# Eight modulation vectors of the first layer: half of their products moved from VectorE to TensorE

## The chip, the cores and the metric

The kernel runs on one core of a Trainium2 chip. The metric is device time in microseconds: the median over several executions of one launch. An engine is named as in the profile: PE is TensorE's matmul, PEld its weight load, DVE is VectorE, ACT is ScalarE, POOL is GpSimd, SP is SyncE, which only issues DMAs here.

## The reference

Two transformer-like blocks of two layers each run one after the other on x, 256 tokens by 1024 channels, all in float32. What matters here is the beginning of the first block. From a conditioning vector c (1024 numbers) it makes, per layer, six vectors of 1024 that shift, scale and gate the activations:

```python
c_act = jax.nn.silu(c)
for layer in range(DEPTH):
    mod = c_act @ ada_w[layer] + ada_b[layer]
    shift1, scale1, gate1, shift2, scale2, gate2 = jnp.split(mod[:, None, :], 6, axis=-1)
    h = rms_norm(x, norm_mix[layer]) * (1.0 + scale1) + shift1
    ...
    y = mixer_conv_hgrn(h, w_in_ab[j], ...)
```

`ada_w[layer]` is 1024 x 6144, so each of the six vectors is the product of a vector with a 1024 x 1024 matrix. `scale1` and `shift1` of layer 0 are needed before anything else of the network can start: the first projection (`w_in_ab`) takes h.

## The kernel before, in words

The activations lie transposed, 8 blocks of 128 channels (partitions) by 256 tokens. All weights come as a stream of 1 MB units, 128 x 2048 float32, in an order written out by `weight_plan`; six buffers `raw` take them. SP issues the loads in that order (`pump`), each when its buffer is given back (`release`), so a late release also holds up every load behind it. An ordinary weight unit is split in two before use: ACT rounds it to `wh` (type fp32r), DVE subtracts to get the rest `wl` (line 314), and PE does three products for each pair of blocks with the activations, which are split likewise into XH and XL (all matmuls stand at line 337, all ACT operations at 294).

The units of `ada_w` are not split. A modulation unit (l, p, h) holds 256 of the 1024 outputs of vector p of layer l; vector 1 is `scale1`, vector 0 is `shift1`, and h counts from 0 to 3. The host lays it out transposed, output on the partition, 1024 inputs along the row, twice (j = 0, 1). `ada_dot` (line 688) multiplies one half by `crow`, c_act spread over all partitions (it lies in the tile adaacc), and sums along the row: one DVE instruction of 128 x 1024 gives one column of 128 outputs, `mod[l, p][:, 2h + j]`, and a tiny one reads the accumulator. `crow` itself is made by PE at the start (`ada_row`).

The stream begins with the eight units of layer 0 that the first projection needs, (0,1,0) to (0,1,3), then (0,0,0) to (0,0,3); the first weight unit, hf 0, goes ahead of the last of them. I call these units 0 to 7. In `layer0_mixer` a loop of eight steps, whose order on DVE and ACT is kept as written, goes through them: step i calls `ada_next()` (both halves of unit i), then `arrived(i)`: for units 0 to 3 ACT scales two blocks by `scale1` (tiles tq, tb), for units 4 to 7 ACT adds `shift1` and rounds to two blocks of XH (tile X); `rest(i)` makes the two blocks of XL on DVE. Before the loop stand the sums of squares on PE (`stats`), the root on ACT (tiles lnvt, rsbt) and two DVE multiplications of x by it (tiles g and sg). In step 7, `unit_hi` puts ACT's rounding of hf 0 (wh) between the XH of unit 6 and that of unit 7. The first projection on PE starts with that wh:

```python
for i in range(8):
    if i == 7:
        lo = self.unit_hi()
    self.ada_next()
    if i:
        rest(i - 1)
    arrived(i)
```

Later modulation units (48 in all) are put between later work in the same way; they are not touched by the change.

Of the kernel before, what the change touches and what calls it, by code (L numbers as in the profile page):

```python
# [10 lines left out]
F32 = mybir.dt.float32  # L11
F32R = mybir.dt.float32r
U8 = mybir.dt.uint8
AF = mybir.ActivationFunctionType
# [9 lines left out]
D = 1024  # L24
NK = D // 128
# [14 lines left out]

DMALO = ()
S5SEQ = "g P0 P1 g T0 T1 TB0 M0 P2 P3 TB1 Q0 Q1 T2 T3 g Q2 Q3"


# [2 lines left out]
def weight_plan():  # L49
    plan = []  # L50

    def cols(key, name, index, c0, n):
        for u in range(n // 256):
            plan.append(("w", (key, u), ("cols", name, index, [(c0 + u * 256, 256)])))

    def rows(key, name, index, r0, n):
        for u in range(n // 256):
            plan.append(("w", (key, u), ("rows", name, index, r0 + u * 256)))

    def ada(l, p):  # L60
        return [("ada", ("ada", l, p, h), ("ada", l, p, h)) for h in range(4)]

    def mlp(tag, w1, w2, l, extra):
        a, b = [], []
        for u in range(DFF // 256):
            a.append(("w", (tag + "a", u), ("cols", w1, l, [(u * 256, 256)])))
            b.append(("w", (tag + "b", u), ("rows", w2, l, u * 256)))
        if tag in COLS2:
            plan.extend(a + [("w", (tag + "b", u), ("tcol", w2, l, u // 2, u % 2)) for u in range(len(a))])
            return  # L70
        n = len(a)
        order = [a[0]]
        for u in range(1, n - 1):
            order += [a[u], b[u - 1]]
        order[-1:] = [a[n - 1], b[n - 3]]
        order += [b[n - 2], b[n - 1]]
        extra = list(extra)
        out = []
        for i, o in enumerate(order):
            out.append(o)  # L80
            if i >= 2 and i % 2 == 0 and extra:
                out.append(extra.pop(0))
        plan.extend(out + extra)

    plan.extend(ada(0, 1) + ada(0, 0))
    more = ada(0, 2) + ada(0, 4) + ada(0, 3)
    for i, (n, c0) in enumerate((("hf", 2048), ("hg", 3072), ("hq", 1536), ("hi", 2560),
                                 ("ac", 512), ("ah", 1024), ("ab", 0))):
        for u in range(2):
            plan.append(("w", (n, u), ("cols", "w_in_ab", 0, [(c0 + u * 256, 256)])))  # L90
            if i:
                plan.append(more.pop(0))
    plan.insert(7, plan.pop(8))
    rows("wab", "w_out_ab", 0, 0, D)
    mlp("m1", "mlp_w1", "mlp_w2", 0, ada(0, 5) + ada(1, 1) + ada(1, 0))
    def unit(name, u, w, index, *c):
        plan.append(("w", (name, u), ("cols", w, index, [(x, 256 // len(c)) for x in c])))

    for u in range(2):
        unit("v", u, "w_qkv", 0, 2 * D + u * 256)  # L100
    more = ada(1, 3) + ada(1, 4) + ada(1, 2)
    for i in range(12):
        if i < 8:
            unit("qk", i, "w_qkv", 0, i * 128, D + i * 128)
        elif i < 10:
            unit("v", i - 6, "w_qkv", 0, 2 * D + (i - 6) * 256)
        else:
            plan.append(("w", ("wc", i - 10), ("rows", "w_out_c", 0, (i - 10) * 256)))
        plan.extend(more.pop(0) for _ in range(SBA[i]))
    for i in range(2, 4):  # L110
        plan.append(("w", ("wc", i), ("rows", "w_out_c", 0, i * 256)))
    mlp("m2", "mlp_w1", "mlp_w2", 1, ada(1, 5))
    glu = [("w", ("glu", m), ("cols", "ssm_w_glu_2", 0, [(m * 128, 128), (D + m * 128, 128)])) for m in range(NK)]
    for k in S5SEQ.split():
        plan.append(glu.pop(0) if k == "g" else ("s5", (k[:-1], int(k[-1])), None))
    plan.extend(glu)
    mlp("m3", "mlp_w1_2", "mlp_w2_2", 0, [])
    cols("k", "w_kvf_2", None, 0, D)
    plan.append(("w", ("f", 0), ("fcols",)))
    for n, u in (("fq", 0), ("fv", 0), ("fq", 1), ("fq", 2), ("fq", 3), ("fv", 1), ("fv", 2), ("fv", 3)):  # L120
        unit(n, u, *(("attn_wq_2", 0, u * 256) if n == "fq" else ("w_kvf_2", None, D + u * 256)))
    rows("wo", "attn_wo_2", 0, 0, D)
    mlp("m4", "mlp_w1_2", "mlp_w2_2", 1, [])
    return plan
# [149 lines left out]
class Prog:  # L274
# [122 lines left out]
    def unit_ahead(self, ahead, between=None):  # L397

        last = min(self.used_n + ahead, len(self.wseq) - 1)
        while self.split_n <= last:  # L400
            j = self.wseq[self.split_n]
            if j not in self.slot:
                assert self.split_n > self.used_n, ("not loaded", self.plan[j][1])
                break
            b = self.split_n % len(self.hb)
            raw = self.raw_of(j)
            if self.plan[j][1] in DMALO:
                self.act(self.hb[b], raw, AF.Copy)
                self.release(j)
                lo = self.lb[b]  # L410
                self.act(lo, self.hb[b].bitcast(F32), AF.Copy, scale=-1.0)
                self.nc.gpsimd.dma_start(out=lo, in_=self.a["wst"][self.wpos[j]], accum_op=ADD)
                self.split_n += 1
                continue
            n = 1 + (self.plan[j][1][0] in HALVES)
            parts = [slice(i * 2048 // n, (i + 1) * 2048 // n) for i in range(n)]
            for c in parts:
                self.act(self.hb[b][:, c], raw[:, c], AF.Copy)
            if between is not None:
                between()  # L420
                between = None
            for c in parts:
                self.tt(self.lb[b][:, c], raw[:, c], self.hb[b][:, c].bitcast(F32), SUB)
            self.release(j)
            self.split_n += 1
        if between is not None:
            between()
# [76 lines left out]
                wh, wl = (t[:, k, m * 128:(m + 1) * 128] for t in (hv, lv))  # L504
                self.pair(outs[m], wh, wl, self.X2[S][:, k], k == 0, k == NK - 1)

    def rows_mm(self, units, xs, banks, start, stop, evac=None, late=False):

        kt = [(h, l, j) for h, l in units for j in range(2)]
        out = lambda m: self.pb[banks[m // 2]][:, (m % 2) * T:(m % 2 + 1) * T]  # L510
        if evac is not None:
            fin, a, b = evac
        if late:
            for q, m in [(q, m) for q in range(2) for m in range(NK)]:
                h, l, j = kt[q]
                w = h[:, j * D + m * 128:j * D + (m + 1) * 128]
                self.mm(out(m), w, xs[q][0], q == 0 and start and m % 2 == 0, False)
                self.mm(out(m), w, xs[q][1], False, False)
            for q, m in [(q, m) for q in range(2) for m in range(NK)]:
                h, l, j = kt[q]  # L520
                self.mm(out(m), l[:, j * D + m * 128:j * D + (m + 1) * 128], xs[q][0], False, q == 1 and stop and m % 2 == 1)
            return
        for m in range(NK):
            o = out(m)
            for q, (h, l, j) in enumerate(kt):
                c = j * D + m * 128
                xh, xl = xs[q]
                wh, wl = h[:, c:c + 128], l[:, c:c + 128]
                self.mm(o, wh, xh, q == 0 and start and m % 2 == 0, False)
                self.mm(o, wh, xl, False, False)  # L530
                self.mm(o, wl, xh, False, q == len(kt) - 1 and stop and m % 2 == 1)
            if evac is not None and m % 2 == 1:
                for i in (m - 1, m):
                    fin(i, out(i))
                    a(i)
                    if i:
                        b(i - 1)
        if evac is not None:
            b(NK - 1)
# [144 lines left out]
    def ada_dot(self, l, p, m, w):  # L684
# [3 lines left out]
        self.nc.vector.tensor_tensor_reduce(out=w, in0=w, in1=self.crow, scale=1.0 if sc is None else sc, scalar=b, op0=MUL, op1=ADD,  # L688
                                            accum_out=self.mod[l, p][:, m:m + 1])

    def ada_affine(self, l, p, m):
        c = l * 48 + p * 8 + m
        if p not in (1, 4):
            return None, self.adab[:, c:c + 1]
        return self.P["norm_mix" if p == 1 else "norm_mlp", l][:, m:m + 1], self.adn[l, p][:, m:m + 1]

    def ada_next(self, n=2):

        with self.tc.high_priority(offset=-BACK["ada"]):
            for _ in range(n):  # L700
                (l, p, h) = self.ada_todo[0]
                i = self.pos["ada", l, p, h]
                j = self.ada_k % 2
                w = self.raw_of(i)[:, j * D:(j + 1) * D]
                self.ada_dot(l, p, 2 * h + j, w)
                self.ada_k += 1
                if j:
                    self.release(i)
# [243 lines left out]
    def mlp(self, tag, S, finish, side=(), after=None, before=None):  # L952
        n = DFF // 256
        with self.tc.tile_pool(name="pm" + tag, bufs=1) as p:
# [22 lines left out]
            def B(us, fin=None):  # L977
                ws = [self.unit((tag + "b", u), ahead=2 - i) for i, u in enumerate(us)]
                xs = [(hh[u % 3][:, j, :], hl[u % 3][:, j, :]) for u in us for j in range(2)]
                self.rows_mm(ws, xs, yb, us[0] == 0, us[-1] == n - 1, fin, (tag + "b", us[0]) in DMALO)  # L980

            def sides(b):
                self.side_banks = (b, b + 1)
# [847 lines left out]
```

## Time and profile before

| what | value |
|---|---|
| median of 3 runs | 1312.97 us (1312.78 to 1313.27) |
| the profiled execution's own time | 1311.48 us |
| its span, first to last instruction | 1309.7 us |
| PE busy | 1225.6 us, 94% of the span |
| DVE busy | 1021.1 us, 78% |
| ACT busy | 681.8 us, 52% |
| mean granted TensorE clock | 0.98 |

The busy shares are means over stages with different limits. The clock is given in shares of full speed: 1.00 is the level of 2.4 GHz, 0.50 that of 1.2 GHz. A matmul in float32 shows as two records, each with a weight load of its own (8 matmuls are x16 in the trace). In a timeline the first number is the start, the second how long the row lasted, xN how many instructions it merges, and the bracket tells what ended the idle time before it.

### The profile page before, as it was taken

What the parts mean: (1) busy time and instruction counts of PE and PEld (TensorE: products, weight loads), DVE (VectorE), ACT (ScalarE), POOL (GpSimd) and SP (SyncE); (2) the same over time, 40 slices, a digit from 0 to 9 for tenths busy, and PEclk for the clock granted to TensorE, in tenths of its full rate; (3) what the DMA queues carried; (4) which work ended last, traced back from release to release, by engine and by line L of the source; (5) the groups of instructions that cost most, each with busy time, mean ns of one, the idle gap of its engine ahead of it and who ended that gap; (6) DMA issues with size and microseconds to landing.
All of it is one profiled execution on the core that took longest, in us unless ns stands there. A gap on an engine that the chain in (4) does not pass through costs nothing.

```text
span 1309.7 us, 22500 instructions
## 1 busy us (share of the span) xinstructions
PE 1225.6 (94%) x9412; PEld 1138.2 (87%) x9412; DVE 1021.1 (78%) x1398; ACT 681.8 (52%) x884; POOL 85.5 (7%) x73
## 2 busy tenths in 40 slices
PE   2999999999999999978889789999999999999997
PEld 2999899999988899978889579887889999888886
DVE  6899999985899969979956857676657786887553
ACT  4545465555548857534555345544545554655442
POOL 0012120000100001000000204000000000100000
PEclk7899999999999999989999899999999999999999
DMA  9867467778365567667579895444555533455520
GB/s 382 325 259 287 201 253 274 279 276 297 131 243 212 205 242 248 249 212 253 180 265 233 233 336 210 160 162 172 214 193 193 193 130 114 156 185 189 213 77 33
DMA packets 63654, 283.84 MB, mean 217 GB/s; under 512 B 8000, under 2 KB 25920, under 8 KB 31936
## 3 DMA queue, kind: packets, MB, share of 16 engines
q1 hardware_dynamic: 63552, 282.40, 60.6%
q8 instruction: 74, 1.21, 0.4%
q14 instruction: 28, 0.23, 0.0%
HBM read 267.70 MB, written 14.68 MB: 216 GB/s over the span
## 4 chain that ended last, share of the span: by engine, by line
PE 68%; DVE 16%; ACT 8%; DMA 4%; issue 3%; POOL 1%; DVEq 0%; ACTq 0%; SPq 0%; POOLq 0%
PE psall L337 67%; DVE wl L314 6%; ACT wh L294 5%; DVE raw L688 2%; DMA raw<-dK 2%; DMA raw<-in_wst_dram 1%; PE psall L340 1%; DMA raw<-dP 1%; DVE tmpn L327 1%; DVE sqt L327 1%; DVE X L327 1%; DVE td L314 1%; POOL sqat L566 1%; DVE sqt L314 0%; ACT X L294 0%
## 5 line engine op out<-in xcount | busy, mean ns | idle before, releaser
L337 PE MATMUL psall<-X,wh 128*128 128x256 f32 (+2 forms) x3360 | 729.3, 308 | 39.7 <-ACT wh L294 23.3
L337 PEld LDWEIGHTS psall<-X,wh 128*128 128x128 f32 x3360 | 544.6, 192 | 78.8 <-ACT wh L294 24.0
L337 PE MATMUL psall<-X,wl 128*128 128x256 f32 (+1 forms) x1992 | 559.2, 284 | 5.9 <-DVE wl L314 5.9
L314 DVE TENSOR_TENSOR wl<-raw,wh 128x2048 fp32r<-128x2048 f32 (+1 forms) x232 | 426.6, 1856 | 108.7 <-ACT wh L294 108.3
L294 ACT ACTIVATE wh<-raw 128x2048 fp32r<-128x2048 f32 (+1 forms) x232 | 354.3, 1546 | 217.3 <-PE psall L337 193.4
L337 PEld LDWEIGHTS psall<-X,wl 128*128 128x128 f32 x1992 | 378.0, 190 | 12.1 <-DVE wl L314 11.3
L337 PE MATMUL psall<-hh,wh 128*128 128x256 f32 x512 | 144.5, 287 | 4.4 <-ACT hh L294 4.3
L337 PE MATMUL psall<-hl,wh 128*128 128x256 f32 x512 | 145.6, 285 | 1.0 <-DVE hl L314 0.9
L337 PE MATMUL psall<-hh,wl 128*128 128x256 f32 x512 | 145.0, 284 | 0.0
L337 PE MATMUL psall<-hid,wh 128*128 128x512 f32 (+1 forms) x432 | 136.3, 372 | 0.0
L566 POOL TENSOR_TENSOR sqat<-sqat,sqt 128x256 f32<-128x256 f32 x52 | 56.2, 1081 | 1054.0 <-ACT sqt L294 1052.9
L337 PE MATMUL psall<-hid,wl 128*128 128x256 f32 x384 | 108.2, 282 | 0.2 <-DVE wl L314 0.2
L337 PEld LDWEIGHTS psall<-hh,wh 128*128 128x128 f32 x512 | 98.0, 193 | 5.6 <-ACT hh L294 5.1
L337 PEld LDWEIGHTS psall<-hl,wh 128*128 128x128 f32 x512 | 98.5, 192 | 1.5 <-DVE hl L314 1.5
L337 PEld LDWEIGHTS psall<-hh,wl 128*128 128x128 f32 x512 | 98.6, 193 | 0.4 <-issue 0.4
L337 PEld LDWEIGHTS psall<-hid,wh 128*128 128x128 f32 x432 | 78.1, 189 | 15.3
L688 DVE CUSTOM_DVE_ANT_0 raw<-raw,adaacc,prmt 128x1024 f32<-128x1024 f32 x64 | 81.4, 1294 | 0.0
L337 PEld LDWEIGHTS psall<-hid,wl 128*128 128x128 f32 x384 | 72.8, 189 | 0.6 <-DVE wl L314 0.6
L294 ACT ACTIVATE tmpn<-psall 128x256 f32<-128x256 f32 (+1 forms) x38 | 17.7, 465 | 62.1 <-PE psall L337 62.1
L314 DVE TENSOR_TENSOR tmpn<-tmpn,psall 128x256 f32<-128x256 f32 (+1 forms) x32 | 17.6, 552 | 38.0 <-ACT tmpn L294 38.0
L688 DVE CUSTOM_DVE_ANT_0 raw<-raw,adaacc,adn 128x1024 f32<-128x1024 f32 x32 | 42.3, 1340 | 4.4 <-ACT td L294 4.4
L294 ACT ACTIVATE ht<-ht 128x512 f32<-128x512 f32 x64 | 40.0, 626 | 6.2 <-DVE ht L327 5.3
(344 smaller groups left out, 1239.6 us busy)
## 6 DMA issues: line engine op xcount, KB each, us to landing
raw<-in_wst_dram SPq DMA_DIRECT2D x231, 1024.0 KB, 4.9
dQ<-s5X SPq DMA_DIRECT2D x8, 512.0 KB, 5.1
dP<-s5X SPq DMA_DIRECT2D x16, 256.0 KB, 3.9
s5X<-in_wst_dram SPq DMA_DIRECT2D x4, 1024.0 KB, 14.8
raw<-dK SPq DMA_DIRECT2D x32, 128.0 KB, 8.4
s5X<-in_s5blk_dram SPq DMA_DIRECT2D x8, 256.0 KB, 3.5
s5X<-dP SPq DMA_DIRECT2D x2, 1024.0 KB, 8.1
raw<-dP SPq DMA_DIRECT2D x2, 1024.0 KB, 12.0
```

Of the source, the lines that this page charges most:

```text
L294: i = self.nc.scalar.activation(out=out, in_=in_, func=func, **kw)
L314: return self.nc.vector.tensor_tensor(out=out, in0=a, in1=b, op=op)
L327: return self.nc.vector.scalar_tensor_tensor(out=out, in0=a, scalar=s, in1=b, op0=op0, op1=op1)
L337: return self.in_bank(out, self.nc.tensor.matmul(out, lhsT=l, rhs=r, start=start, stop=stop))
L340: return self.in_bank(out, self.nc.tensor.transpose(out, in_, self.ident))
L566: self.nc.gpsimd.tensor_tensor(out=self.sqa, in0=self.sqa, in1=s, op=ADD)
L688: self.nc.vector.tensor_tensor_reduce(out=w, in0=w, in1=self.crow, scale=1.0 if sc is None else sc, scalar=b, op0=MUL, op1=ADD, accum_out= ...
```

## The change

Units 0, 2, 4 and 6, that is h = 0 and h = 2 of vectors 1 and 0 of layer 0, go to PE. The host lays them out like ordinary weights, 8 blocks of 128 inputs by 256 outputs. For each half, `ada_mm` does eight float32 matmuls, the weights 128 x 128, the moving operand one column of `cact`, summed in one column of PSUM bank 5, and an ACT instruction of 128 x 1 brings the sum to `mod` with the same scale and bias that `ada_dot` used. Units 1, 3, 5 and 7 stay on DVE. The lines on `DMALO` and `late` remove code that did not run, since `DMALO` was empty.

```diff
-DMALO = ()
+ADAPE = {(0, p, h) for p in (0, 1) for h in (0, 2)}
...
     def ada(l, p):
-        return [("ada", ("ada", l, p, h), ("ada", l, p, h)) for h in range(4)]
+        return [("ada", ("ada", l, p, h), ("cols", "ada_w", l, [(p * D + h * 256, 256)]) if (l, p, h) in ADAPE
+                 else ("ada", l, p, h)) for h in range(4)]
...
+    def ada_mm(self, l, p, m, w):
+
+        sc, b = self.ada_affine(l, p, m)
+        o = self.pb[5][:, 8 * p + m:8 * p + m + 1]
+        for k in range(NK):
+            self.mm(o, w[:, k, :], self.cact[:, k:k + 1], k == 0, k == NK - 1)
+        self.act(self.mod[l, p][:, m:m + 1], o, AF.Identity, scale=sc, bias=b)
+
...
                 j = self.ada_k % 2
-                w = self.raw_of(i)[:, j * D:(j + 1) * D]
-                self.ada_dot(l, p, 2 * h + j, w)
+                if (l, p, h) in ADAPE:
+                    self.ada_mm(l, p, 2 * h + j, self.raw_of(i).rearrange("p (k c) -> p k c", c=256)[:, :, j * 128:(j + 1) * 128])
+                else:
+                    self.ada_dot(l, p, 2 * h + j, self.raw_of(i)[:, j * D:(j + 1) * D])
```

How the instructions stand on two engines shows what waits for what. The first place is PE between the sums of squares (td, tw) and the first projection (X, wh). Before:

```order
L337 MATMUL psall<-td,onesd 128x256 [waits Activation_49] x4
L337 MATMUL psall<-tw,onesd 128x256 [waits Activation_49] x4
L337 MATMUL psall<-X_171,wh_73 128x256 [waits Activation_49]
L337 MATMUL psall<-X_171,wh_73 128x256 [waits DVE_49]
L337 MATMUL psall<-X_171,wh_73 128x256 x3
```

And now (raw_67 is the buffer of unit 0, raw_69 that of unit 2, raw_71 that of unit 4; lines are shifted by one):

```order
L338 MATMUL psall<-td,onesd 128x256 [waits Activation_49] x4
L338 MATMUL psall<-tw,onesd 128x256 [waits Activation_49] x4
L338 MATMUL psall<-cact,raw_67 128x1 [waits DMAHW3_49]
L338 MATMUL psall<-cact,raw_67 128x1 x7
L338 MATMUL psall<-cact,raw_67 128x1 [waits Activation_49]
L338 MATMUL psall<-cact,raw_67 128x1 x7
L338 MATMUL psall<-cact,raw_69 128x1 [waits DMAHW5_49,Activation_49]
L338 MATMUL psall<-cact,raw_69 128x1 x7
L338 MATMUL psall<-cact,raw_69 128x1 [waits Activation_49]
L338 MATMUL psall<-cact,raw_69 128x1 x7
L338 MATMUL psall<-cact,raw_71 128x1 [waits DMAHW7_49,Activation_49]
```

Eight groups of eight matmuls now stand there, two to a unit, and from the second on each group waits for an ACT instruction, the one that reads the group before it out of the same PSUM bank.

The second place is ACT from the root to the rounding of hf 0 (wh_73). Before:

```order
L294 ACTIVATE lnvt<-psall,epscols 128x256 [waits PE_49]
L294 ACTIVATE rsbt<-lnvt 128x256 [waits Activation_49]
L307 ACT_TABLE_LOAD
L294 ACTIVATE tq<-g_181,mod_1_117 128x256 [waits DVE_49]
L294 ACTIVATE tq<-g_181,mod_1_117 128x256
L294 ACTIVATE tq<-g_181,mod_1_117 128x256 [waits DVE_49] x2
L294 ACTIVATE tb<-sg,mod_1_117 128x256 [waits DVE_49] x4
L294 ACTIVATE X_171<-tq,mod_0_116 128x256 [waits DVE_49,Activation_49] x4
L294 ACTIVATE X_171<-tb,mod_0_116 128x256 [waits DVE_49,Activation_49] x2
L294 ACTIVATE wh_73<-raw_68 128x2048 [waits DMAHW2_49]
```

And now, from the root on:

```order
L295 ACTIVATE mod_1_117<-psall,adn_1_128,prmt 128x1 [waits PE_49]
L295 ACTIVATE rsbt<-lnvt 128x256 [waits Activation_49]
L308 ACT_TABLE_LOAD
L295 ACTIVATE mod_1_117<-psall,adn_1_128,prmt 128x1 [waits PE_49]
L295 ACTIVATE tq<-g_181,mod_1_117 128x256 [waits DVE_49]
L295 ACTIVATE tq<-g_181,mod_1_117 128x256 [waits Activation_49]
L295 ACTIVATE tq<-g_181,mod_1_117 128x256 [waits DVE_49] x2
L295 ACTIVATE mod_1_117<-psall,adn_1_128,prmt 128x1 [waits PE_49] x2
L295 ACTIVATE tb<-sg,mod_1_117 128x256 [waits Activation_49] x2
L295 ACTIVATE tb<-sg,mod_1_117 128x256 [waits DVE_49] x2
L295 ACTIVATE mod_0_116<-psall,prmt 128x1 [waits PE_49] x2
L295 ACTIVATE X_171<-tq,mod_0_116 128x256 [waits Activation_49] x2
```

The first of the new instructions, for unit 0, stands ahead of rsbt; the pair for unit 2 stands behind all four tq; a further pair, for unit 6, stands behind the four X of tq, and the two X of tb and wh_73 follow it. On DVE the dots of units 0, 2, 4 and 6 are gone and the rest keeps its order: g and sg, then units 1, 3 and 5, four XL, unit 7, four XL, then wl. On SP the loads keep their order; those that reuse the buffers of units 0, 2, 4 and 6 now wait for PE where they waited for DVE.

## Rows read from the trace of the kernel before

**Rows 1.** The page: span, busy time, PE and its clock in 40 slices.

```profile
span 1309.7 us, 22500 instructions
...
PE 1225.6 (94%) x9412; PEld 1138.2 (87%) x9412; DVE 1021.1 (78%) x1398; ACT 681.8 (52%) x884; POOL 85.5 (7%) x73
...
PE   2999999999999999978889789999999999999997
...
PEclk7899999999999999989999899999999999999999
```

**Rows 2.** The chain that ended last, 14 to 36 us: start, us, what.

```profile
14.27 0.48 ACT lnvt L294
...
14.77 0.42 ACT rsbt L294
...
15.22 1.23 DVE g L314
...
33.30 0.51 ACT X L294
33.81 1.81 ACT wh L294
...
35.66 0.58 PE psall L337
```

**Rows 3.** The groups of instructions on DVE, 0 to 36 us.

```profile
L688 DVE CUSTOM_DVE_ANT_0 raw<-raw,adaacc,adn 128x1024 f32<-128x1024 f32 x8 | 10.3, 1343 | 4.4 <-ACT td L294 4.4
L688 DVE CUSTOM_DVE_ANT_0 raw<-raw,adaacc,prmt 128x1024 f32<-128x1024 f32 x8 | 9.9, 1281 | 0.0
```

**Rows 4.** The timeline of ACT, 9 to 38 us.

```profile
20.15 0.51 ACT L294 ACTIVATE tq<-g,mod 128x256 f32<-128x256 f32 x1 [0.76 <-DVE mod L688]
```

**Rows 5.** The timeline of PE, 0 to 90 us.

```profile
3.89 3.75 PE L337 MATMUL psall<-cstt,cact 128*128 128x128 f32 x16 [3.89 <-DVE lbt L314]
...
35.66 6.13 PE L337 MATMUL psall<-X,wh 128*128 128x256 f32 x34 [21.43 <-ACT wh L294]
41.63 2.17 PE L337 MATMUL psall<-X,wl 128*128 128x256 f32 x17
```

**Rows 6.** Busy time by stretch: start and end, length, engines, clock, DMA share, GB/s.

```profile
core 0: us, PE busy (x) PEld busy (x) DVE busy (x) ACT busy (x) POOL busy (x), PEclk, DMA share, GB/s
12.50:19.30 6.80, 1.73 (x8) 1.17 (x7) 4.08 (x5) 3.50 (x6) 0.00 (x0) 1.00 1.01 422
19.30:35.60 16.30, 0.00 (x0) 0.00 (x0) 16.30 (x29) 7.47 (x14) 0.00 (x0) 0.50 1.01 420
35.60:39.80 4.20, 4.14 (x19) 4.14 (x20) 4.20 (x7) 3.70 (x5) 0.00 (x0) 0.50 1.01 415
39.80:45.00 5.20, 5.20 (x46) 5.20 (x45) 5.20 (x5) 2.10 (x3) 0.00 (x0) 1.00 0.85 335
...
613.20:616.60 3.40, 1.70 (x18) 1.44 (x19) 3.35 (x4) 2.57 (x5) 0.00 (x0) 1.00 0.99 326
616.60:620.00 3.40, 3.40 (x18) 3.40 (x17) 3.40 (x4) 0.60 (x1) 0.00 (x0) 0.50 0.77 319
```

**Rows 7.** The timeline, 363 to 364.8 us.

```profile
363.37 0.53 PEld L337 LDWEIGHTS psall<-onesd,sqat 128*128 128x128 f32 x4
363.48 0.50 PE L337 MATMUL psall<-onesd,sqat 128*128 128x1 f32 x4
```

**Rows 8.** The groups of weight loads, 35.6 to 39.8 us.

```profile
L337 PEld LDWEIGHTS psall<-X,wh 128*128 128x128 f32 x20 | 4.2, 324 | 21.8 <-ACT wh L294 21.8
```

**Rows 9.** Weight loads and matmuls of tiles cact, onesd: ns min/median/max, first and last start.

```profile
L337 PEld LDWEIGHTS psall<-cstt,cact x16: 286/333/334, 3.9 to 7.0; 128*128 128x128 f32 x16
L337 PE MATMUL psall<-cstt,cact x16: 421/421/551, 3.9 to 7.2; 128*128 128x128 f32 x16
...
L337 PEld LDWEIGHTS psall<-onesd,sqat x8: 187/190/192, 363.4 to 1005.9; 128*128 128x128 f32 x8
```

**Rows 10.** The groups of instructions on ACT, whole span.

```profile
L294 ACT ACTIVATE rtokt<-psall,epscols 128x2 f32<-128x2 f32 x2 | 0.5, 258 | 0.0
```

More of the change, by code (lines that the diff above doesn't have):

```diff
@@ L406, in unit_ahead @@
             raw = self.raw_of(j)
[L407 to L414, printed above, removed]
             n = 1 + (self.plan[j][1][0] in HALVES)
@@ L505, in proj_2, with rows_mm @@
                 self.pair(outs[m], wh, wl, self.X2[S][:, k], k == 0, k == NK - 1)
-    def rows_mm(self, units, xs, banks, start, stop, evac=None, late=False):
+    def rows_mm(self, units, xs, banks, start, stop, evac=None):
         kt = [(h, l, j) for h, l in units for j in range(2)]
@@ L512, in rows_mm @@
             fin, a, b = evac
[L513 to L522, printed above, removed]
         for m in range(NK):
@@ L979, in B @@
                 xs = [(hh[u % 3][:, j, :], hl[u % 3][:, j, :]) for u in us for j in range(2)]
-                self.rows_mm(ws, xs, yb, us[0] == 0, us[-1] == n - 1, fin, (tag + "b", us[0]) in DMALO)
+                self.rows_mm(ws, xs, yb, us[0] == 0, us[-1] == n - 1, fin)
             def sides(b):
```

## The prediction

> **What bounds the kernel now.** I read the page first [rows 1]: PE is busy 94% of a span of 1309.7 us, and its row of slices reads 9 nearly everywhere except in the first slice (2). So whatever moves the beginning of PE's stream moves the end by about as much. The first projection starts on PE at 35.66 us [rows 2]; what happens before it is the stage that the change touches. The chain of waits through that stage [rows 2] goes from the sums of squares on PE over the root on ACT (lnvt from 14.27, rsbt to 15.19) to DVE, which does g and sg (from 15.22) and then one dot after the other: units 1 to 6 stand on this chain, DVE has no gap between 19.3 and 35.6 us [rows 6], and the dots cost 1.34 us (vector 1) and 1.28 us (vector 0) each [rows 3]. Last come the second X of unit 6 on ACT (33.30), the rounding of hf 0 (33.81, 1.81 us) and PE. So DVE's dots bound the opening. The DMA runs at 420 GB/s there [rows 6], 2.5 us per unit, also about DVE's pace; it is ahead of DVE by the buffers that it has already filled.
>
> Then I looked at what PE's clock does [rows 6]: 1.00 from 12.5 to 19.3 us, 0.50 from 19.3 to 39.8, where PE does nothing until 35.66, and 1.00 after that.
>
> **What the change removes.** Eight dots leave DVE: four of 1.34 and four of 1.28 us, 10.5 us busy. Two of the eight (unit 0) ran in DVE's idle time before g and gave nothing to the chain, so at best the chain would lose 7.9 us. It loses that only if PE delivers the other half in time.
>
> **What it adds.** Eight groups of eight float32 matmuls, 16 records each, and eight ACT instructions. The order puts them in a strict row: a group waits for ACT to have read the group before. So the cost that counts is the latency of one round: group, hop, ACT, hop.
>
> *ACT.* The nearest row reads two columns of PSUM: 258 ns [rows 10]. With two hops of 0.04 us (as between X, wh and PE in the chain [rows 2]) that is 0.34 us.
>
> *A group at the upper clock level.* The matmuls of 128 x 1 in [rows 7] are the same form: their four weight loads take 0.53 us, the last 0.19 of it [rows 9], so one follows another after 0.113 us, and the four records last 0.50 us. Sixteen: 12 x 0.113 + 0.50 = 1.85 us; a round is 2.2 us.
>
> *A group at the lower level.* The nearest row is the first group of the kernel, also 8 float32 matmuls, also 128 x 128 weights, 128 columns instead of 1: 16 records in 3.75 us [rows 5]. Its weight loads took 333 ns, against 190 of the 128 x 1 form, and the very first, with nothing in front of it, 286 [rows 9]; where 0.50 was granted they took 324 [rows 8]. So the loads themselves are slower there, and I expect loads, not columns, to set the pace: 3.75 us a group, a round of 4.1 us. The bounds are 1.85 us (as at the upper level) and 3.75.
>
> The Trainium skill, "TensorE: Matmul & The Clock Gate", section "LDWEIGHTS (loading the stationary operand)", gives the load as columns divided by 1.2 GHz at either level, which by its formula is an estimate of 0.107 us a record. By that a group would cost about the same at both levels, and this is the third case below. The rows of 286 and 324 against 190 ns speak against it.
>
> *Which level holds.* No row shows a stretch of one-column matmuls alone. From 613.2 to 616.6 us PE was at work for 1.70 of 3.40 us, at 1.00, and in the next stretch 0.50 was granted [rows 6]: work with gaps did not hold the level there. The new groups wait for ACT in every round, and in them PE spends its time on loads. So I take the lower level from about 19.3 us on, as before.
>
> **The sum.** Unit 0 starts behind the sums of squares, at about 14.1, at the upper level: first group to 15.95, its `mod` on ACT to 16.25. That stands ahead of the root's second step: rsbt ends at 16.7 instead of 15.19, and g, sg and unit 1 on DVE, which keep their lengths, move with it. From the end of rsbt to the end of the fourth tq (20.15 + 0.51 [rows 4]) was 5.5 us; the fourth tq now ends at 22.15. Meanwhile PE has done unit 0's second group (to 18.1) and unit 2's first (to 21.5, partly at the lower level), but the `mod` of the latter stands behind the fourth tq: 22.45. From there five rounds are in a row, the second group of unit 2 and both of units 4 and 6: 5 x 4.1 = 20.4 us, to 42.85. ACT fits its tb and X of units 3 to 5 into these rounds, DVE's units 1, 3 and 5 are done long before. Then two X (1.02 us), wh (1.85 with the hop) and PE: 45.7 instead of 35.66, **10.1 us later**.
>
> What could hide or add to this: the loads that wait for PE now (units 6 and 7, hg 0 and hg 1) are given free later, at 18.1, 26.5, 34.6 and 42.8 us, but at 2.5 us each every one lands before its use, which moves as well, so I cost them at nothing. If the DMA lost that lead, a late unit would cost 2.5 us. DVE has slack now, but its order is fixed and its next work (XL, wl) waits for X and wh. PE starts hf 0 at the lower level as before, so that cost stays. What follows starts from PE and keeps its order, so the shift reaches the end. The profiled execution took 1311.48 us, 1.8 more than its span, and that rest is not touched: 1311.48 + 10.1 = 1321.6. It lies 1.5 us under the median of 1312.97, so the median becomes **1323.1 us**.
>
> **The rivals.**
>
> 1. *The clock holds* (not slower). Since PE is never idle for long between 14 and 43 us, the one-column matmuls might count as work enough. The Trainium skill's same page, section "Why this matters for your kernels", asks for no idle gaps between bursts to keep the level; by that rule this is what would happen. For it: the clock stayed at 1.00 from 12.5 to 19.3 although PE was busy for 1.73 of 6.80 us [rows 6]. Against it: 613.2 to 616.6, above. Worked out: five rounds of 2.2 end at 33.4, with X and wh PE starts at 36.2 (+0.55), but at the upper level: 34 matmuls that took 5.97 us (35.66 to 41.63 [rows 5]) take 34 x 5.20/46 = 3.85 us [rows 6], -2.1. Together -1.6: 1311.4 us. It decides between the rounds of 4.1 and of 2.2: with the clock up, a round under about 2.5 us makes the change no loss.
> 2. *The lower level comes earlier* (slower still). Before, the clock came up shortly before 12.5 us, from the sums of squares: the first group of the kernel still ran long loads [rows 9]. If it comes up only behind them, unit 0 runs at the lower level too: first `mod` at 18.15, rsbt 18.6, fourth tq 24.1, unit 2's first round to 26.3, five rounds to 46.75, PE at 49.6: +14.0, 1327.0 us.
> 3. *The load keeps its pace at the lower level.* Then a group is 15 x 0.113 plus the last load's lag and one matmul at that level, 0.42 [rows 9], some 2.2 us, a round 2.5; five end at 35.0 and PE starts at 37.8: +2.2, 1315.2 us.
>
> That the change does not do what it says can be left out: the order shows the groups and the missing dots.
>
> **How the numbers follow.** Forecast 0.70, rival 1 0.13, rival 2 0.12, rival 3 0.05. The forecast's own width: a group of 3.4 instead of 3.75 us takes 1.8 off, the moment at which the clock comes up behind hf 0 gives or takes 2, longer hops (0.1 each) add 1: 1319 to 1326. Taking in rival 2 with its own 2 us gives 1318 to 1329, which leaves 0.18 out. About 0.2%, 2.6 us, is what a measurement of this kernel can tell from no change. Slower by more: forecast and rival 2, 0.82. Within it: rival 3 and most of rival 1, 0.14. Faster by more: the rest of rival 1, 0.04.
>
> **What would show it.** In the profile of the changed kernel: PE's first projection at about 45.7 us; eight groups of 16 records of 128 x 1 between 14 and 43 us, the last five about 4.1 us apart, with weight loads above 300 ns; granted clock 0.50 from 19 us into the first projection; rsbt about 1.5 us later; DVE with some 17 us of gaps before 46 us. I am wrong if these groups run at 1.00, if their loads follow each other after 0.11 us at 0.50, or if the first projection is late by 10 us and the end is not, which would mean that a stage behind it had been waiting for something that does not move with it.

## The result, and the profile after

| | before | after |
|---|---|---|
| median | 1313.12 us (6 runs, 1310.97 to 1316.02) | 1324.09 us (6 runs, 1323.32 to 1326.64) |
| ratio | | 1.0084, 95% interval 1.0068 to 1.0101 |
| profiled execution | 1311.48 us, clock 0.980 | 1326.64 us, clock 0.971 |

The change makes the kernel slower by 11.0 us (8.9 to 13.3), or 0.8%. (The eight "vectors" of the title are the eight units of two vectors.) The forecast was 1323.1 us, on a median of 1312.97. The page of the changed kernel, the counterpart of [rows 1]:

```profile
span 1324.9 us, 22743 instructions
...
PE 1254.7 (95%) x9540; PEld 1166.9 (88%) x9540; DVE 1012.6 (76%) x1382; ACT 682.9 (52%) x892; POOL 84.7 (6%) x73
...
PE   7899999999989999979889789999999999999997
...
PEclk7799999999999999989999889999999999999999
```

PE's first slice went from 2 to 7: the change put work where PE stood idle. Only the 128 new records were added, but PE's busy time rose by 29 us. The timeline of PE, as in [rows 5], shows most of it: the eight groups add up to 24.8 us (start, length, what; the bracket is the idle time before and what ended it):

```profile
13.88 1.84 PE L338 MATMUL psall<-cact,raw 128*128 128x1 f32 x16
16.17 1.95 PE L338 MATMUL psall<-cact,raw 128*128 128x1 f32 x16 [0.44 <-ACT mod L295]
18.56 3.13 PE L338 MATMUL psall<-cact,raw 128*128 128x1 f32 x16 [0.44 <-ACT mod L295]
22.18 3.57 PE L338 MATMUL psall<-cact,raw 128*128 128x1 f32 x16 [0.49 <-ACT mod L295]
26.19 3.57 PE L338 MATMUL psall<-cact,raw 128*128 128x1 f32 x16 [0.44 <-ACT mod L295]
30.12 3.58 PE L338 MATMUL psall<-cact,raw 128*128 128x1 f32 x16 [0.35 <-ACT mod L295]
...
37.97 3.58 PE L338 MATMUL psall<-cact,raw 128*128 128x1 f32 x16 [0.35 <-ACT mod L295]
44.49 6.66 PE L338 MATMUL psall<-X,wh 128*128 128x256 f32 x34 [2.95 <-ACT wh L295]
50.99 2.18 PE L338 MATMUL psall<-X,wl 128*128 128x256 f32 x17
```

The first group takes 1.84 us, the last five 3.57 to 3.58. Each waits 0.35 to 0.49 us for ACT to have read the one before, and the first projection starts at 44.49 us instead of 35.66. Busy time by stretch, as in [rows 6] (PEclk is the third number from the right), shows the level that holds there:

```profile
16.00:18.00 2.00, 1.83 (x16) 1.83 (x16) 1.55 (x2) 1.70 (x3) 0.00 (x0) 1.00 0.99 414
18.00:20.00 2.00, 1.56 (x11) 1.47 (x11) 2.00 (x4) 1.15 (x3) 0.00 (x0) 0.77 1.03 426
20.00:22.50 2.50, 2.01 (x10) 1.93 (x10) 2.50 (x5) 1.26 (x3) 0.00 (x0) 0.50 1.01 419
...
26.00:30.00 4.00, 3.57 (x16) 3.48 (x16) 0.29 (x2) 1.93 (x6) 0.00 (x0) 0.50 0.77 276
...
44.40:49.00 4.60, 4.51 (x21) 4.51 (x22) 4.13 (x4) 4.43 (x5) 0.00 (x0) 0.50 0.81 328
49.00:52.00 3.00, 3.00 (x24) 3.00 (x24) 3.00 (x2) 0.00 (x0) 0.00 (x0) 0.87 0.94 347
```

The lower level, 1.2 GHz, holds from about 19 us until hf 0 is well under way. DVE, which bounded this stage, is now busy for 0.29 of 4.00 us (26 to 30). The chain of waits, the counterpart of [rows 2], has turned over:

```profile
15.76 0.35 ACT mod L295
16.11 0.31 ACT rsbt L295
...
16.45 1.23 DVE g L315
...
21.38 0.51 ACT tq L295
21.89 0.25 ACT mod L295
...
37.97 3.59 PE psall L338 x16
...
41.58 0.26 ACT mod L295
41.84 0.79 ACT X L295 x2
42.64 1.81 ACT wh L295
...
44.49 5.59 PE psall L338 x25
```

Up to 21.89 us it still runs over ACT and DVE as before, with `mod` of unit 0 ahead of rsbt; from there to 41.84 every piece is a PE group or the ACT instruction that reads it. The durations of the tile cact (minimum, median, maximum in ns), to be read beside [rows 9]:

```profile
L338 PEld LDWEIGHTS psall<-cact,raw x128: 186/333/338, 13.7 to 41.1; 128*128 128x128 f32 x128
L338 PE MATMUL psall<-cact,raw x128: 167/352/373, 13.9 to 41.2; 128*128 128x1 f32 x128
```

The loads have both of the durations seen before: about 190 ns at one level and 333 at the other.

**From the opening to the end.** Matching every PE instruction behind the opening with its twin in the trace of before, the shift is 8.83 us at the first projection, 9.38 behind hf 0 (more of hf 0 ran at the lower level), and stays there until about 139 us. Then it grows in steps to 15.2 at the end. The first step is a stretch in which only the changed kernel's execution fell to the lower level; the same work, about 9.4 us earlier, in before:

```profile
135.00:140.00 5.00, 5.00 (x45) 5.00 (x44) 5.00 (x6) 1.24 (x2) 2.37 (x1) 1.00 0.01 3
```

and in the changed kernel:

```profile
145.00:149.00 4.00, 4.00 (x23) 4.00 (x23) 4.00 (x4) 0.85 (x1) 2.35 (x1) 0.57 0.02 4
```

PE is busy throughout in both. So 9.4 us of the profiled difference of 15.2 come from the opening, and 5.8 from such later stretches. The profiled execution is the slowest of the six; that the later falls differ between executions of one kernel is likely, but each kernel has only one profile. Of the seven experiments below, the profiles of two (units 0 and 2 only, every product twice) show a fall at this same work and five don't. The interval of the medians, 8.9 to 13.3 us, holds the 9.4.

### The profile page after: what moved, and what is told of

The parts are those of the page before. It is cut to its first block, busy times and chain, and to the rows that moved or that the text cites. A ratio compares the mean times of both kernels' runs of the same rounds, so it can differ in the third digit from the quotient of the medians.

```text
span 1324.9 us, 22743 instructions
## 1 busy us (share of the span) xinstructions
PE 1254.7 (95%) x9540; PEld 1166.9 (88%) x9540; DVE 1012.6 (76%) x1382; ACT 682.9 (52%) x892; POOL 84.7 (6%) x73
## 3 DMA queue, kind: packets, MB, share of 16 engines
q8 instruction: 75, 1.23, 0.4%
## 4 chain that ended last, share of the span: by engine, by line
PE 69%; DVE 15%; ACT 8%; issue 3%; DMA 3%; POOL 1%; DVEq 0%; ACTq 0%; POOLq 0%; SPq 0%
PE psall L338 68%; DVE wl L315 6%; ACT wh L295 5%; DMA raw<-dK 2%; DVE raw L671 1%; DMA raw<-in_wst_dram 1%; PE psall L341 1%; DVE tmpn L328 1%; DVE sqt L328 1%; DVE td L315 1%; POOL sqat L549 1%; DVE sqt L315 1%; DVE X L328 1%; ACT X L295 0%; DVE tmpn L315 0%
## 5 line engine op out<-in xcount | busy, mean ns | idle before, releaser
L671 DVE CUSTOM_DVE_ANT_0 raw<-raw,adaacc,prmt 128x1024 f32<-128x1024 f32 x60 | 77.1, 1305 | 0.0
L671 DVE CUSTOM_DVE_ANT_0 raw<-raw,adaacc,adn 128x1024 f32<-128x1024 f32 x28 | 37.0, 1335 | 0.0
## 6 DMA issues: line engine op xcount, KB each, us to landing
s5X<-in_wst_dram SPq DMA_DIRECT2D x4, 1024.0 KB, 14.4
```

## The experiments

The open question was what makes a group cost 3.58 us: the clock that one-column matmuls are granted, or the strict row with ACT's wait in it. Seven kernels tell this apart; all differ from the changed kernel by what is shown. With each stands the moment at which the first projection starts (35.66 before, 44.49 after the change) and the median with its ratio to the kernel before, timed beside it (1313.08 us for "both" and the two kernels with units 1, 3 and 5, 1314.06 for the other four).

One thing differs between these profiles that no edit touches. In the profiles of before, the change, the wide kernel and "both", the first eight records of the sums of squares (tile td) took about 3.78 us, in the other five 1.99, so that PE was through with the sums at 12.2 to 12.8 us there, instead of 13.9 to 14.4. Moments from the two sorts of profile can be compared only to within that.

### The moving operand 128 columns wide

```diff
-        o = self.pb[5][:, 8 * p + m:8 * p + m + 1]
+        g = 2 * (m // 4) + m % 2
+        o = self.pb[5][:, 128 * g:128 * g + 128]
         for k in range(NK):
-            self.mm(o, w[:, k, :], self.cact[:, k:k + 1], k == 0, k == NK - 1)
-        self.act(self.mod[l, p][:, m:m + 1], o, AF.Identity, scale=sc, bias=b)
+            self.mm(o, w[:, k, :], self.cact[:, k:k + 1].to_broadcast([128, 128]), k == 0, k == NK - 1)
+        self.act(self.mod[l, p][:, m:m + 1], o[:, 0:1], AF.Identity, scale=sc, bias=b)
```

> The moving operand of the new matmuls is the same column of cact repeated 128 times, the output 128 equal columns of which ACT reads one; groups, bank and waits on PE are those of the change, and on ACT the root's second step now stands ahead of the first mod. My theory (the price is the clock level: a group is paced by its weight loads, 0.113 us a record at 1.00 and 0.213 at 0.50, so 128 columns cost nothing more, and work of this width lets 1.00 be granted): groups of about 1.85 us, rounds of 2.2, first projection on PE at about 35 us instead of 44.5, its first matmuls at 1.00, total about 1310 us. Rival (a group is dear because float32 weight loads from a fresh buffer are dear at any level, and the clock does not matter): groups stay at 3.6 us, first projection at about 43, total about 1322. Second rival (more columns make each record longer): groups over 4 us, total above 1325.

First projection at 36.79 us, median 1314.5, ratio 1.0003 (0.9991 to 1.0015). PE's timeline of this kernel:

```profile
19.60 2.05 PE L338 MATMUL psall<-cact,raw 128*128 128x128 f32 x16 [0.44 <-ACT mod L295]
...
31.80 2.05 PE L338 MATMUL psall<-cact,raw 128*128 128x128 f32 x16 [0.35 <-ACT mod L295]
36.79 5.85 PE L338 MATMUL psall<-X,wh 128*128 128x256 f32 x34 [2.94 <-ACT wh L295]
```

and its stretches:

```profile
24.00:29.00 5.00, 4.21 (x34) 3.72 (x32) 1.26 (x4) 2.20 (x6) 0.00 (x0) 1.00 1.01 408
29.00:34.00 5.00, 4.15 (x33) 3.72 (x32) 4.14 (x8) 2.23 (x7) 0.00 (x0) 1.00 1.02 393
34.00:39.00 5.00, 2.21 (x10) 2.21 (x11) 2.71 (x5) 5.00 (x7) 0.00 (x0) 0.79 0.96 385
```

128 equal columns do 128 times the products, and a group takes 2.05 us instead of 3.58, with the same wait for ACT in every round: the level is 1.00 throughout. That wins back 7.7 of the 8.8 us at the first projection, although on ACT the first `mod` now stands behind rsbt and the second group starts at 17.11 instead of 16.17 us. The total came out 4 us above what was expected: the projection starts 1.8 us later than I put it (groups of 2.05 us instead of 1.85, and that later second group), and the level falls behind PE's wait of 2.94 us for wh, just as hf 0 begins (at 36.9 us, by the 0.79 of 34 to 39), so that the first part of hf 0 runs at 0.50 once more.

### One column, but without the wait for ACT

```diff
-        o = self.pb[5][:, 8 * p + m:8 * p + m + 1]
+        g = 2 * (m // 4) + m % 2
+        o = self.pb[(2, 3, 5, 6)[g]][:, 8 * p + m:8 * p + m + 1]
```

> One column as in the change, but the four groups of a vector go to four PSUM banks (2, 3, 5, 6), so that PE no longer waits for ACT between most groups; the order on all engines is that of the change. Theory (a round is 3.58 us of group and 0.35 us of waiting, and the fourth group also waited from 21.7 to 22.2 behind a tq): the lower level stays, the groups follow each other every 3.4 us, the last ends at about 36 to 37 us instead of 41.6, first projection at about 39.5, total about 1319 us. Rival (the waits for ACT are what costs, and without gaps on PE the clock holds at 1.00): groups of 1.85 us back to back, limited by the loads, first projection at about 33, total about 1309.

First projection at 39.70 us, median 1321.72, ratio 1.0046 (1.0030 to 1.0061). The theory's moment came true; its total was 2.7 us too low. PE's timeline:

```profile
8.57 1.99 PE L338 MATMUL psall<-td,onesd 128*128 128x256 f32 x8 [0.99 <-ACT td L295]
...
12.13 24.63 PE L338 MATMUL psall<-cact,raw 128*128 128x1 f32 x128
39.70 6.99 PE L338 MATMUL psall<-X,wh 128*128 128x256 f32 x34 [2.94 <-ACT wh L295]
```

and two stretches:

```profile
14.00:19.00 5.00, 5.00 (x30) 5.00 (x29) 4.30 (x5) 3.59 (x7) 0.00 (x0) 0.61 1.01 421
19.00:24.00 5.00, 5.00 (x25) 5.00 (x25) 5.00 (x9) 1.60 (x5) 0.00 (x0) 0.50 1.01 416
```

All 128 records stand in one row without a gap. The records count PE as busy for 5.00 of 5.00 us, its loads too, and 0.50 is granted, from about 15 us on. So the gaps are not what costs the level here. The Trainium skill, "TensorE: Matmul & The Clock Gate", section "Why this matters for your kernels", asks for no idle gaps between bursts of matmuls, to avoid drops; there are none in this row and the level dropped all the same, so here that is not enough. For thin matmuls the same section offers two ways, to loop over all blocks of K or to pad. This kernel does the first without a wait and is granted 0.50; padding from 1 column to 128, in the experiment before, held 1.00.

The level fell at 15 us here and at 19 in the change, and that doesn't come from the missing gaps: it came up earlier too, as the td row shows, which in the change reads

```profile
8.48 3.78 PE L338 MATMUL psall<-td,onesd 128*128 128x256 f32 x8 [0.99 <-ACT td L295]
```

In two kernels that do wait for ACT and whose td row took 1.99 us as well (units 0 and 2 only, every product twice) it fell at 15.6 and 14.8 us. For the same reason the groups begin at 12.13 us here and at 13.88 in the change. So of the 4.8 us by which the first projection comes earlier, 1.8 belong to the execution, and about 3.0 to the banks. The medians say about the same: 11.0 us over the kernel before for the change, 7.7 here.

### Both

```diff
-        o = self.pb[5][:, 8 * p + m:8 * p + m + 1]
+        g = 2 * (m // 4) + m % 2
+        o = self.pb[(2, 3, 5, 6)[g]][:, 0:128]
         for k in range(NK):
-            self.mm(o, w[:, k, :], self.cact[:, k:k + 1], k == 0, k == NK - 1)
-        self.act(self.mod[l, p][:, m:m + 1], o, AF.Identity, scale=sc, bias=b)
+            self.mm(o, w[:, k, :], self.cact[:, k:k + 1].to_broadcast([128, 128]), k == 0, k == NK - 1)
+        self.act(self.mod[l, p][:, m:m + 1], o[:, 0:1], AF.Identity, scale=sc, bias=b)
```

> Units 0, 2, 4, 6 on PE as in the change, with both edits: 128 equal columns and four PSUM banks. Theory (at 1.00 a group is 1.95 to 2.05 us, and without the waits the eight follow each other from about 14): the last ends at about 30 us, first projection at about 33, 3 us before the run with the wide operand alone (36.8) and 2.5 before the kernel before the change; total about 1310 us. Rival (by then the loads of the units, 2.5 us each, or ACT's row set the pace): first projection at about 36 as with the wide operand alone, total about 1314.

First projection at 32.31 us, median 1311.09, ratio 0.9986 (0.9968 to 1.0004), close to the theory; the total can't be told from before. PE's timeline:

```profile
13.70 10.88 PE L338 MATMUL psall<-cact,raw 128*128 128x128 f32 x96
25.56 3.81 PE L338 MATMUL psall<-cact,raw 128*128 128x128 f32 x32 [0.98 <-DMA raw<-in_wst_dram]
```

and a stretch of it, the twin of the one at 0.61 above:

```profile
14.00:19.00 5.00, 5.00 (x47) 5.00 (x47) 4.14 (x5) 3.95 (x8) 0.00 (x0) 1.00 1.01 419
```

The same banks, the same loads, PE just as busy, and 1.00 instead of 0.61: on PE the width is the only edit (on ACT rsbt stands ahead of the first `mod`, as in the wide kernel). That it isn't a matter of one profile shows in the mean granted clock of every execution: in the 36 of the three kernels with wide operands it is 0.979 to 0.987, in the 39 of the five with one column (the change among them) 0.962 to 0.978. No run tried a width between 1 and 128. Sixteen records now take 1.8 us, and for the first time PE waits for a transfer: the stream of units is the next bound.

### Units 0 and 2 only

```diff
-ADAPE = {(0, p, h) for p in (0, 1) for h in (0, 2)}
+ADAPE = {(0, 1, 0), (0, 1, 2)}
```

> Half of the change undone: only units 0 and 2 (scale1) go to PE, units 4 and 6 (shift1) are back on DVE. Theory (the path is DVE's g, sg, units 1 and 3, then 4 and 5, one pair of XL, unit 6; PE's four groups end at about 25.8 us and their mod is used from there): first projection at about 34.5 us, 1.2 us earlier than before the change and 10 earlier than with it, at 0.50 as before; total about 1312 us. Rival (any PE group costs its full 3.9 us on the path): half of the change's loss remains, first projection at about 40, total about 1318.

First projection at 34.10 us, median 1313.28, ratio 0.9991 (0.9983 to 1.0000). The theory held, but 1.4 us by which the sums of squares ended sooner than in before belong to the execution, so the gain of 1.6 at the projection isn't shown to be the edit's. Its four groups take 1.84, 2.99, 3.57 and 3.57 us, against 1.84, 1.95, 3.13 and 3.57 in the change, where the level fell a group later. They lie beside DVE's dots of units 1, 3, 4 and 5, which last until 27.45 us; DVE then waits 0.90 us for the X that hangs on the last group, so little of their price reaches the chain. The price depends on how far such groups outlast DVE's own work.

### Every product twice

```diff
-        for k in range(NK):
+        for k in [*range(NK), *range(NK)]:
```

> The suspected cost doubled: every group does its eight matmuls twice, the second time over the first, the output is the same. Order on all other engines as in the change. Theory (loads at 0.50 are on the path): each of the five rounds grows by 3.4 us, the groups before by some 9 together, first projection at about 70 us, total about 1350 us. Rival (hops, ACT and the wait between engines are the cost): the total grows by less than 5 us. Second rival (longer groups let the clock rise): groups of about 3.6 us, first projection at about 47, total about 1326.

First projection at 71.04 us, median 1350.43, ratio 1.0269 (1.0252 to 1.0286), as the theory had it. PE's timeline of two groups:

```profile
16.81 6.98 PE L338 MATMUL psall<-cact,raw 128*128 128x1 f32 x32 [0.44 <-ACT mod L295]
24.24 6.98 PE L338 MATMUL psall<-cact,raw 128*128 128x1 f32 x32 [0.44 <-ACT mod L295]
```

6.98 us for 32 records against 3.58 for 16: a record costs (6.98 - 3.58) / 16 = 0.213 us at 0.50. With width and banks together it was 10.88 / 96 = 0.113 us at 1.00. PE's groups bound the opening, and the end moved by 36.4 us where the projection moved by 35.4.

### Units 1, 3 and 5 instead, wide, in four banks

```diff
-ADAPE = {(0, p, h) for p in (0, 1) for h in (0, 2)}
+ADAPE = {(0, 1, 1), (0, 1, 3), (0, 0, 1)}
...
-        o = self.pb[5][:, 8 * p + m:8 * p + m + 1]
+        g = 2 * (m % 8 // 4) + m % 2
+        o = self.pb[(2, 3, 5, 6)[g]][:, 0:128]
         for k in range(NK):
-            self.mm(o, w[:, k, :], self.cact[:, k:k + 1], k == 0, k == NK - 1)
-        self.act(self.mod[l, p][:, m:m + 1], o, AF.Identity, scale=sc, bias=b)
+            self.mm(o, w[:, k, :], self.cact[:, k:k + 1].to_broadcast([128, 128]), k == 0, k == NK - 1)
+        self.act(self.mod[l, p][:, m:m + 1], o[:, 0:1], AF.Identity, scale=sc, bias=b)
```

> Another choice of units: 1, 3 and 5 go to PE (128 equal columns, four banks), unit 0 goes back into DVE's idle time before g, and unit 6, which decides over wh, and unit 7 are on DVE. Theory (PE done with three units at about 26 us, DVE's path is g, sg, units 2, 4, 6 and two pairs of XL): first projection at about 29 us, 6 to 7 before the kernel before the change; total about 1307 us. Rival (the stream of units at 2.5 us each bounds it: unit 7 is the ninth and cannot be there before about 27.5, its last products, X and wl come behind it): PE starts early but stalls within hf 0, total about 1310 to 1312.

First projection at 31.22 us, median 1310.72, ratio 0.9976 (0.9960 to 0.9991): faster than both kernels. Unit 0 goes back into DVE's idle time, so rsbt no longer stands behind a `mod`. The theory's 29 us were not reached; the rival's bound was right. DVE's timeline:

```profile
19.92 1.28 DVE L671 CUSTOM_DVE_ANT_0 raw<-raw,adaacc,prmt 128x1024 f32<-128x1024 f32 x1 [1.88 <-DMA raw<-in_wst_dram]
...
26.33 1.28 DVE L671 CUSTOM_DVE_ANT_0 raw<-raw,adaacc,prmt 128x1024 f32<-128x1024 f32 x1 [2.55 <-DMA raw<-in_wst_dram]
...
31.30 1.29 DVE L671 CUSTOM_DVE_ANT_0 raw<-raw,adaacc,prmt 128x1024 f32<-128x1024 f32 x1 [1.68 <-DMA raw<-in_wst_dram]
```

and its chain of waits:

```profile
18.06 13.22 DMA raw<-in_wst_dram
...
31.30 1.29 DVE raw L671
```

Units 4, 6 and 7, the three that DVE waits for, come late: neither engine bounds the opening any more, the loads do, at 420 GB/s, the rate they had in before [rows 6].

### The same units with one column

The kernel above with this taken back:

```diff
-        o = self.pb[(2, 3, 5, 6)[g]][:, 0:128]
+        o = self.pb[(2, 3, 5, 6)[g]][:, 0:1]
...
-            self.mm(o, w[:, k, :], self.cact[:, k:k + 1].to_broadcast([128, 128]), k == 0, k == NK - 1)
+            self.mm(o, w[:, k, :], self.cact[:, k:k + 1], k == 0, k == NK - 1)
```

> The same choice of units (1, 3, 5 on PE, four banks) with one column as in the change; order on all engines as in the run with 128 columns. Theory (the clock is at 0.50 from about 15 to 19 us, groups of 3.4 us): unit 5's second group ends at about 33 us, first projection at about 37, total about 1315 us, that is about 8 above its twin with 128 columns, for the sake of the clock alone. Rival (the choice of units is what matters, not the width): within 2 us of the twin.

First projection at 34.52 us, median 1313.73, ratio 1.0004 (0.9990 to 1.0019). PE's timeline:

```profile
12.32 3.63 PE L338 MATMUL psall<-cact,raw 128*128 128x1 f32 x32
17.19 13.59 PE L338 MATMUL psall<-cact,raw 128*128 128x1 f32 x64 [1.24 <-DMA raw<-in_wst_dram]
```

At the upper level 32 records take 3.63 us, 0.113 each; at the lower one 64 take 13.59, 0.212 each. The width is worth 3.0 us in the medians and 3.3 at the projection here, between the 8 of the theory and the rival's 2: the wide twin is held up by the loads, so part of what PE saves is spent waiting for them.

### From the opening to the total

The end of the first 17 matmuls with wl on PE, against before (43.80 us), and the difference of the medians, in us, with the interval of the ratio times the median before:

| kernel | shift in the opening | total |
|---|---|---|
| the change | +9.4 | +11.0 (8.9 to 13.3) |
| wide | +0.9 | +0.4 (-1.2 to 2.0) |
| four banks | +4.9 | +7.7 (3.9 to 8.0) |
| both | -3.6 | -2.0 (-4.2 to 0.5) |
| units 0 and 2 | -1.0 | -0.8 (-2.2 to 0.0) |
| every product twice | +35.9 | +36.4 (33.1 to 37.6) |
| units 1, 3, 5, wide | -3.6 | -2.4 (-5.3 to -1.2) |
| units 1, 3, 5, one column | -1.4 | +0.7 (-1.3 to 2.5) |

In seven of the eight the shift of the opening lies in the interval of the total, in the last just outside. In the five kernels whose sums of squares ran at the upper level (four banks, units 0 and 2, every product twice, and both with units 1, 3 and 5) up to 2 us of the shift can be the execution's own, so the two columns agree to about 2 us and not better. The medians give no sign of another place that moves with the change; single executions of one kernel differ by several us (before: 1306.91 to 1317.67), and in the profiles the clock falls at later places.

## Why the prediction was right

**The row of rounds** held: the last five groups stand one behind the other, with ACT between, and set the first projection. A round was put at 4.1 us and measured 3.9 to 4.0: the group took 3.58 instead of 3.75 (in the row that I took it from [rows 5], with 128 columns at the lower level, records follow each other after the same 0.213 us; the step behind the first is 0.11 and the last record 0.07 longer), ACT and its hops 0.35 to 0.44 instead of 0.34.

**The start of the row** held: rsbt ended at 16.42 (put at 16.7), the fourth tq at 21.89 (22.15). The price of `mod` ahead of rsbt came out a little smaller than worked out: g started 1.23 us later than in [rows 2], where the sum had 1.5.

**The end of the row**: the first projection came at 44.49, 1.2 us before the 45.7 of the sum. Five rounds gave 0.7 of this, the start 0.3, and the two X overlapped (0.79 instead of 1.02). Then hf 0 took 0.55 more than before, because the clock rose about 5.3 us into it (0.87 in 49 to 52 us is 0.8 us at the lower level) instead of 4.1 [rows 6]; the sum had that cost unchanged. Together 9.4 instead of 10.1.

**The end of the kernel** moved with the opening, as forecast. The profiled execution was 5.0 us above the 1321.6 of the sum, though its opening was 0.7 below: the later clock falls. The medians, which average over them, differ by 11.0. The loads that wait for PE, which the sum put at nothing, did cost nothing: the DMA slowed to 236 to 289 GB/s between 26 and 42 us, but no transfer stands on the chain from 15.76 us to the first projection, and PE goes from wh to wl without a gap. That the forecast of 1323.1 lies within a microsecond of 1324.09 owes something to two small errors with opposite signs.

**Rival 1, the clock holds**, fell: the groups ran at 0.50, and the kernel with no gaps at all did too. Its support, 6.80 us at 1.00 with PE busy for 1.73 [rows 6], spoke only of the stretch to 19 us, and there the level did hold. But its arithmetic was good: with the clock held by wide operands, the round was 2.4 to 2.5 us, the break-even that it named, and that kernel measured 1.0003 of before.

**Rival 2, the lower level already for unit 0**, is not in the profiled execution: the first two groups took 1.84 and 1.95 us. It supposed that the level comes up late, only behind the sums of squares; no profile shows that. In the kernels with four banks, with units 0 and 2, and with every product twice the level fell early (14.8 to 15.6 us), but there it had come up before the sums; in the others it came up during them.

**Rival 3, loads that keep their pace**, fell: 0.213 us from one record to the next at 0.50 against 0.113 at 1.00, and 333 against 190 ns for the load. The Trainium skill, "TensorE: Matmul & The Clock Gate", section "LDWEIGHTS (loading the stationary operand)", has a formula that names no clock level. The estimate of 0.107 us by it is near the 0.113 of the upper level and misses the lower one.

DVE's idle time is larger than the 17 us I named: 11.3 before g, and 8.1, 3.8 and 1.7 before its XL. The last three cost nothing, since DVE bounds nothing behind 21.4 us now. The six dots that could have left the chain are 7.8 us, not 7.9; nothing hangs on it.

## What to carry to other kernels

In this kernel a product with a vector on PE cost its weight loads, and these followed the clock: 1.8 us per 128 outputs of a 1024-long float32 product at 1.00, 3.6 at 0.50. What helped was to make the moving operand wide by repeating the column, and to give the sums banks of their own; both together moved the first projection by 12.2 us, though the edits add nothing but redundant products. Before handing work to an idle engine, ask where the other engine is the bound. With one column, units 1, 3 and 5 instead of 0, 2, 4 and 6 took the loss from 7.7 us to 0.7 (one unit fewer on PE as well); with wide operands the two choices differ by 0.4 us, which is within the noise. And ask what bounds next: with wide operands the loads did, and the gain over before was 2.4 us at best (1.2 to 5.3).

## What the runs showed of the hardware

Records that show PE busy for 5.00 of 5.00 us, with loads back to back, went with a granted clock of 0.50; the same loads with 128 columns behind each kept 1.00, even with gaps (4.15 of 5.00 busy). The busy share of the records could not have told the level here. A weight load of one shape takes 190 ns at one level and 333 at the other within one kernel, and the spacing goes from 0.113 to 0.213 us: a float32 product with one column is slowed by the clock almost in full. Width adds nothing to the spacing: with 128 columns the records follow each other after 0.113 us at 1.00 ("both") and after 0.213 at 0.50 (the first group of the kernel before). It lengthens the end of a group alone (2.05 against 1.84 us at 1.00).

The profile's clock row can mislead at the very start: between 8 and 12 us of the changed kernel's profile it reads 1.00, while the loads of td took 337 ns. There the durations of the loads tell the level.

The granted clock also falls at places where PE is busy throughout (0.57 from 145 to 149 us of the changed kernel's profile, 1.00 for the same work in before). Why it does so in one profile and not in another wasn't tried.
